# A hybrid encoder block: the memory branch's fourth gate unit moves from the attention phase into the last memory head

## The chip, the cores and the metric

The kernel runs on one core of a Trainium2 chip. The core has five engines with instruction queues of their own: TensorE (PE, matmuls, with its weight loads shown apart as PEld), VectorE (DVE), ScalarE (ACT), GpSimd (POOL) and SyncE (SP, which here only starts transfers). They meet through semaphores. The metric is the device time of one execution in microseconds.

## The reference

The block takes x (1024 tokens, 1024 channels) and a fixed memory of 256 rows. It normalises x and projects it with one wide matrix into everything that follows. Three mixers run side by side, and each is widened with a gate:

```python
h = rms_norm(x, g_pre[layer])
a_qkv, bq, bk, bv, mq, ga, gb, gm, mg = jnp.split(h @ w_in[layer], split_at, axis=-1)
# oa: dilated sliding-window attention, 3 groups x 8 heads of 64
# ob: grouped-query attention, 8 query heads on 2 key heads, softmax over all 1024 keys
sm = jnp.einsum('bshd,bnhd->bhsn', mq.reshape(b, s, M_HEADS, M_HEAD_DIM), km).astype(jnp.float32)
pm = jax.nn.softmax(sm * (M_HEAD_DIM ** -0.5), axis=-1).astype(dt)
om = jnp.einsum('bhsn,bnhd->bshd', pm, vm).reshape(b, s, M_Q)
ya = (oa * jax.nn.silu(ga)) @ w_br_a[layer]
yb = (ob * jax.nn.silu(gb)) @ w_br_b[layer]
ym = (om * jax.nn.silu(gm)) @ w_br_m[layer]
gates = jax.nn.sigmoid((mg + b_merge[layer]).astype(jnp.float32)).astype(dt).reshape(b, s, N_BRANCHES, d)
merged = gates[:, :, 0] * ya + gates[:, :, 1] * yb + gates[:, :, 2] * ym
x = x + rms_norm(merged @ w_out[layer], g_post[layer])
```

The change concerns silu(gm): 512 gate channels of the memory branch, worked out as four units of 128 channels.

## The kernel before

Every float32 matmul is done in three passes. A number is split into a high part (names ending in h) and the rest (ending in l), and high x high, high x low and low x high are added up in PSUM. ACT makes the high part by a copy and DVE the low part by a subtraction (the helper `split`, L105 and L106).

A dense unit projects all 1024 tokens to 128 output channels. It is two halves of 512 tokens, and each half is 24 matmuls of 128x512 (L143, L145, L147), so a unit has 48. Its weights are one transfer of 512 KB (L114), split by ACT (wh) and DVE (wl). A half goes to one of two PSUM tiles named d, and an evacuation empties it. The evacuation of a gate unit (`add_gate`) is a multiplication on DVE (L220), a tanh on ACT (L221), a multiplication on DVE (L222) and a transfer of 256 KB to memory (L223). A filler unit (`add_filler`) has one DVE multiplication (L212), one tanh and one transfer.

The dense units stand in one queue. `weave` takes the next so many units and runs them between the steps of an attention generator. It compares the shares of dense work and attention work that are done, by costs written into the code, and yields to the one that is behind (with a factor called lead). This fixes the order of PE's instructions when the program is built. The other engines' orders come from a scheduler with priorities, and are fixed then too. Each engine works through its own list in order.

The phases, in time: the start with the key and value projections, up to 60 us; the memory phase (M) up to about 225 us; phase B, the grouped-query attention, up to 572 us; phase A, the dilated attention, up to 1150 us; then the merge and the output projection.

In the memory phase `m_att(h)` handles head h of four. Its tokens come in four steps n of 256. A step n has, on PE, the scores (6 matmuls of 128x256 into s), on DVE a minimum (L581) and a small multiplication (L582), on ACT two exponentials (L584), on DVE a reciprocal (L587) and two scalings of pm (L589), then on PE four transposes of pm (L597), a split of the result into mph (ACT) and mpl (DVE), and last 6 matmuls into ov, which ACT copies to om (L611) and SP stores to od. The transposes follow the scores by two steps, the ov matmuls by three. The queries of a head are the tiles mqh and mql, one buffer each.

Phase B opens with `b_const`, on POOL: it writes KB (128 partitions x 2048), from ones (L672, 4 partitions) and from KS (L673, 64 partitions), and a small tile `one` (L674). KB belongs to a pool that lies where the memory phase's pool was, so its first write waits until the tiles there have been read for the last time. `b_att` then runs 16 blocks of 8 steps. A step has on PE one matmul for a row maximum (L688, to tr), two for scores (L706, L707) and two for the product with the values (L727, L728). DVE reduces tr to bn (L689) and makes bpl (L106), ACT makes the exponentials bp (L709) and bph, and POOL sums bp into bl (L716, L718). Once a block DVE makes bnm (L691), PE transposes it (L696), and DVE writes a part of QL from it (L697). With all that go 16 dense units before the change: nine gate units and seven fillers.

Of the kernel before, what the change touches and what calls it, by code (L numbers as in the profile page):

```python
# [50 lines left out]
def block(ctx: ExitStack, tc: tile.TileContext, x, xT, memT, cst, msk, bcst, tabA, gpost,  # L51
# [27 lines left out]
    def pss1():  # L79
        return bank["p"].tile([P, 512], F32, name="s1", tag="s1", bufs=bank["n"][1])  # L80

    def pst():
        return bank["p"].tile([P, 4, 128], F32, name="tr", tag="t", bufs=bank["n"][2])

    def pso():
        return bank["p"].tile([P, 512], F32, name="ov", tag="o", bufs=bank["n"][3])
# [17 lines left out]
    def split(dst_h, dst_l, src):  # L104
        A.activation(dst_h, src, AF.Copy)  # L105
        V.tensor_tensor(dst_l, src, dst_h.bitcast(F32), op=OP.subtract)  # L106
# [3 lines left out]
    def load_w(src, n=1024):  # L110
        if extra:
            extra.append(extra.pop(0))
        raw = (extra[0] if extra else wp).tile([P, 1024], F32, name="wr", bufs=WR)
        nc.sync.dma_start(raw[:, :n], src)  # L114
        wh = wp.tile([P, 1024], R, name="wh")
        wl = wp.tile([P, 1024], R, name="wl")
        split(wh[:, :n], wl[:, :n], raw[:, :n])
        k = n // 128
        return (wh[:, :n].rearrange("p (k f) -> p k f", k=k),
                wl[:, :n].rearrange("p (k f) -> p k f", k=k))  # L120

    def passes(out_ps, terms):
        n = len(terms)
        for i, (a, b) in enumerate(terms):
            PE.matmul(out_ps, a, b, start=i == 0, stop=i == n - 1)  # L125
# [24 lines left out]
    queue = []  # L150
    ready = {}

    early = {}
# [9 lines left out]
    def run_items(count):  # L163
        for _ in range(count):
            n = done[0]
            prepare(n)
            prepare(n + 1)
            yield from queue[n][1](ready.pop(n))
            done[0] += 1

    def cost_items(count):
        return sum(q[2] for q in queue[done[0]:done[0] + count])

    def weave(count, att=None, att_cost=0.0, lead=1.0, prio=ATT_PRIO):
        dg = run_items(count)
        dc = cost_items(count)
        d = a = 0.0
        live_d, live_a = True, att is not None
        while live_d or live_a:
            if live_d and (not live_a or a / att_cost >= min(1.0, d / dc * lead)):  # L180
                try:
                    d += next(dg)
                except StopIteration:
                    live_d = False
                    d = 1e18
            else:
                try:
                    with tc.high_priority(offset=prio):
                        a += next(att)
                except StopIteration:  # L190
                    live_a = False
# [3 lines left out]
    def add_unit(src, evac):  # L195
        def gen(w):
            for half in range(2):
                p = psd()
                yield from dense(w, half, p)
                evac(half, p)  # L200
        queue.append((lambda: load_w(src), gen, UNIT))
# [15 lines left out]
    def add_gate(i, p_):  # L217
        def evac(half, p):
            th = fp["p"].tile([P, 512], F32, name="fth", bufs=2)
            V.tensor_tensor(th, p, rb[:, half * 512:half * 512 + 512], op=OP.mult)  # L220
            A.activation(p, th, AF.Tanh, scale=0.5)  # L221
            V.scalar_tensor_tensor(th, p, 1.0, th, op0=OP.add, op1=OP.mult)  # L222
            nc.sync.dma_start(g2d[i, p_, :, half * 512:half * 512 + 512], th)  # L223
        add_unit(wu[U_G + 4 * i + p_], evac)
# [13 lines left out]
    def close(p):  # L238
        p.__exit__(None, None, None)
# [327 lines left out]
    def m_att(h):  # L567
        qh, ql = MQ[h]
        for _ in range(4):
            yield 250  # L570
        st = {}

        def scores(n):
            sv = pss1().rearrange("p (t k) -> p t k", t=2)
            nm = mt_.tile([P, 2], F32, name="mnm", bufs=3)
            l = mt_.tile([P, 2], F32, name="mls", bufs=3)
            pm = mt_.tile([P, 2, 256], F32, name="pm", bufs=2)
            for j in range(2):
                t = slice((2 * n + j) * 128, (2 * n + j) * 128 + 128)
                passes(sv[:, j], [(qh[:, t], kmh[:, h]), (qh[:, t], kml[:, h]), (ql[:, t], kmh[:, h])])  # L580
            V.tensor_reduce(nm, sv, axis=AX.X, op=OP.min)  # L581
            V.tensor_tensor(nm, nm, rcol[:, 2 * n:2 * n + 2], op=OP.mult)  # L582
            for j in range(2):
                A.activation(pm[:, j], sv[:, j], AF.Exp, scale=nrcol[:, 2 * n + j:2 * n + j + 1], bias=nm[:, j:j + 1],  # L584
                             accum_out=l[:, j:j + 1])
            rl = mt_.tile([P, 2], F32, name="mrl", bufs=4)
            V.reciprocal(rl, l)  # L587
            for j in range(2):
                V.tensor_scalar(pm[:, j], pm[:, j], rl[:, j:j + 1], None, op0=OP.mult)  # L589
            st[n] = pm  # L590

        def trans(n):
            pm = st[n]
            tp = pst().rearrange("p (k t) q -> p k t q", k=2)
            for kt in range(2):
                for j in range(2):
                    PE.transpose(tp[:, kt, j, :], pm[:, j, kt * 128:kt * 128 + 128], ident)  # L597
            ph = mt_.tile([P, 2, 256], R, name="mph", bufs=2)
            pl = mt_.tile([P, 2, 256], R, name="mpl", bufs=2)
            split(ph, pl, tp.rearrange("p k t q -> p k (t q)"))  # L600
            st[n] = (ph, pl)

        def pv(n):
            ph, pl = st.pop(n)
            o = pso()
            terms = []
            for kt in range(2):
                terms += [(vmh[:, kt, h], ph[:, kt]), (vmh[:, kt, h], pl[:, kt]), (vml[:, kt, h], ph[:, kt])]
            passes(o[:, 0:256], terms)
            om = mt_.tile([P, 256], F32, name="om", bufs=2)  # L610
            A.activation(om, o[:, 0:256], AF.Copy)  # L611
            nc.sync.dma_start(od[2, h, :, n * 256:n * 256 + 256], om)

        for n in range(7):
            if n < 4:
                scores(n)
            yield 654
            if 0 <= n - 2 < 4:
                trans(n - 2)
            yield 436  # L620
            if 0 <= n - 3 < 4:
                pv(n - 3)
            yield 654

    M_COST = 1000.0 + 7 * (654 * 2 + 436.0)
# [3 lines left out]
    mq_unit(2)  # L629
    mq_unit(3)  # L630
    add_gate(2, 2)
    early[len(queue)] = lambda: load_w(wu[U_G + 11])
    weave(1)
    weave(2, m_att(0), M_COST, 1.2)
    weave(2, m_att(1), M_COST, 1.2)
    weave(1, m_att(2), M_COST, 1.0)
    weave(1, m_att(3), M_COST, 1.0)
    close(mtp)
    close(mbp)
    close(mlp)  # L640
# [4 lines left out]
    with tc.tile_pool(name="ba", bufs=1, reuse_waits="tile") as ba:  # L645
# [137 lines left out]
        ng = 0  # L783
        for i in (2, 1, 0):
            for p_ in range(4):
                if (i, p_) not in ((2, 0), (2, 1), (2, 2)):
                    add_gate(i, p_)
                    ng += 1
        for j in FILL_B:
# [324 lines left out]
    with tc.tile_pool(name="mg", bufs=1, reuse_waits="tile") as mg:  # L1114
# [78 lines left out]
        for m in range(len(steps) + 2):  # L1193
            if m < len(steps):
                n, i, f = steps[m]
                ths[m] = mg_unit(i, f)
            if m >= 2:
                n, i, f = steps[m - 2]
# [87 lines left out]
U_G = 36  # L1286
# [112 lines left out]
```

## Time and profile before

| what | us |
|---|---|
| median of 3 runs | 1531.39 (1531.35 to 1532.13) |
| the profiled execution | 1529.17 |
| its span, first to last instruction | 1527.2 |
| PE busy in the span | 1493.5 (98%) |
| DVE busy | 966.0 (63%) |
| ACT busy | 713.5 (47%) |
| POOL busy | 429.8 (28%) |

The granted clock of TensorE was 0.997 of its full speed in the mean of the profiled execution. A matmul of 128x512 has a duration of 0.40 us in the records but starts 0.23 us after the one before, since matmuls are pipelined; where work is counted here, the distance of the starts is used. In the lists of the profile a line gives the engine, the line of the kernel, the operation, the output and inputs by name, and their sizes. A bracket or an arrow names what an idle engine waited for. An engine's durations include the time in which a started instruction is held up.

### The profile page before, as it was taken

Reading aid. Unit: us, or ns where it says so; the run is one execution under the profiler, and the core shown is the slowest. Engines: PE = TensorE matmul, PEld = TensorE weight load, DVE = VectorE, ACT = ScalarE, POOL = GpSimd, SP = SyncE. Lnnn points to the kernel's source line nnn. Section 1 sums busy time; section 2 is a strip of 40 time slices with the busy share of each in tenths; the row PEclk is TensorE's granted clock in tenths of the full one; section 3 lists DMA queues with packets and bytes.
Section 4 is the critical chain, followed back from the end, with each engine's and each line's share of the span. In section 5 each row is a group of like instructions: output and inputs, shape, how many; then the busy total and the mean of one; then the engine's idle time right before and its main releaser. Section 6 shows DMA issues by size and latency. Waiting matters only on the chain.

```text
span 1527.2 us, 20804 instructions
## 1 busy us (share of the span) xinstructions
PE 1493.5 (98%) x7748; PEld 1233.9 (81%) x7748; DVE 966.0 (63%) x1602; ACT 713.5 (47%) x1459; POOL 429.8 (28%) x357
## 2 busy tenths in 40 slices
PE   7899989999999999999999999999999999999998
PEld 7799977777777778888878888887888788888787
DVE  7665569999988975555566566556635442524843
ACT  6544345666677661554445445444642111212321
POOL 1425413444444552211221222122200100223422
PEclk9999999999999999999999999999999999999999
DMA  6232011111111112101121121112126541623432
GB/s 233 90 111 70 29 51 57 53 56 49 63 34 60 63 63 87 42 29 43 54 61 43 42 83 45 42 31 83 42 77 195 172 126 35 206 70 117 124 111 97
DMA packets 55044, 119.79 MB, mean 78 GB/s; under 512 B 13792, under 2 KB 23712, under 8 KB 54816
## 3 DMA queue, kind: packets, MB, share of 16 engines
q1 hardware_dynamic: 54800, 118.34, 24.4%
q8 instruction: 61, 1.00, 0.3%
q14 instruction: 39, 0.32, 0.1%
q10 hardware_dynamic: 144, 0.13, 0.0%
HBM read 96.06 MB, written 22.38 MB: 78 GB/s over the span
## 4 chain that ended last, share of the span: by engine, by line
PE 77%; DVE 10%; issue 4%; ACT 4%; POOL 3%; DMA 3%; SPq 0%; DVEq 0%; POOLq 0%; ACTq 0%
PE d L147 12%; PE d L143 12%; PE d L145 12%; PE sc L125 7%; PE sc L1246 4%; PE s L125 3%; PE sc L147 3%; PE sc L143 3%; PE sc L145 3%; PE ov L987 2%; DVE bpl L106 2%; PE ov L728 2%; PE s L707 1%; PE s L706 1%; PE ov L727 1%
## 5 line engine op out<-in xcount | busy, mean ns | idle before, releaser
L143 PE MATMUL d<-hh,wh 128*128 128x512 f32 x992 | 396.4, 400 | 5.2 <-DVE fth L222 5.2
L147 PE MATMUL d<-hh,wl 128*128 128x512 f32 x992 | 397.3, 400 | 0.0
L145 PE MATMUL d<-hl,wh 128*128 128x512 f32 x992 | 393.8, 397 | 0.0
L143 PEld LDWEIGHTS d<-hh,wh 128*128 128x128 f32 x992 | 187.3, 189 | 42.5 <-DVE fth L222 6.5
L147 PEld LDWEIGHTS d<-hh,wl 128*128 128x128 f32 x992 | 187.3, 189 | 39.0 <-issue 4.0
L145 PEld LDWEIGHTS d<-hl,wh 128*128 128x128 f32 x992 | 187.4, 189 | 36.2 <-issue 1.0
L105 ACT ACTIVATE wh<-wr 128x1024 fp32r<-128x1024 f32 (+1 forms) x100 | 95.3, 954 | 245.4 <-PE sc L145 106.0
L718 POOL TENSOR_TENSOR bl<-bl,bp 128x512 f32<-128x512 f32 x96 | 135.8, 1414 | 121.3 <-ACT bp L709 111.2
L836 POOL TENSOR_TENSOR rot<-rot,t2a 128x512 f32<-128x512 f32 x48 | 82.5, 1720 | 297.6 <-DVE t2a L835 297.6
L106 DVE TENSOR_TENSOR bpl<-bp,bph 128x512 fp32r<-128x512 f32 x128 | 131.9, 1031 | 23.6 <-ACT bph L105 23.1
L106 DVE TENSOR_TENSOR wl<-wr,wh 128x1024 fp32r<-128x1024 f32 (+1 forms) x100 | 119.0, 1190 | 21.5 <-ACT wh L105 20.8
L709 ACT ACTIVATE bp<-s 128x512 f32<-128x512 f32 x128 | 76.2, 595 | 59.9 <-PE s L707 57.8
L1147 POOL TENSOR_TENSOR acc<-acc,th 128x1024 f32<-128x1024 f32 x16 | 45.4, 2837 | 201.5 <-DVE th L1146 201.5
L945 ACT ACTIVATE pra<-pra,sts 128x128 f32<-128x128 f32 (+2 forms) x152 | 67.1, 442 | 62.3 <-DVE sts L937 61.6
L689 DVE TENSOR_REDUCE bn<-tr 128x1 f32<-128x512 f32 x128 | 86.5, 680 | 3.8 <-PE tr L688 3.3
L147 PE MATMUL sc<-hh,wl 128*128 128x512 f32 x224 | 87.3, 390 | 1.2 <-DVE wl L106 1.2
L937 DVE CUSTOM_DVE_ANT_0 pra<-s,mask 128x128 f32<-128x128 f32 (+2 forms) x152 | 48.4, 348 | 62.2 <-PE s L125 49.2
L143 PE MATMUL sc<-hh,wh 128*128 128x512 f32 x224 | 87.3, 390 | 0.0
L145 PE MATMUL sc<-hl,wh 128*128 128x512 f32 x224 | 87.1, 389 | 0.0
L105 ACT ACTIVATE bph<-bp 128x512 fp32r<-128x512 f32 x128 | 80.8, 631 | 3.5
L833 DVE TENSOR_TENSOR rot<-d,tab 128x512 f32<-128x512 f32 x48 | 33.1, 689 | 67.4 <-PE d L147 67.1
L125 PE MATMUL sc<-gh,wh 128*128 128x512 f32 x192 | 74.7, 389 | 0.0
(276 smaller groups left out, 3066.0 us busy)
## 6 DMA issues: line engine op xcount, KB each, us to landing
wr<-in_wu SPq DMA_DIRECT2D x76, 512.0 KB
g2d<-fth SPq DMA_DIRECT2D x24, 256.0 KB
wgt<-wgd SPq DMA_DIRECT2D x24, 256.0 KB
ot<-od SPq DMA_DIRECT2D x12, 512.0 KB
gt<-g2d SPq DMA_DIRECT2D x12, 512.0 KB
wr<-in_wbr SPq DMA_DIRECT2D x24, 256.0 KB
thd<-fth SPq DMA_DIRECT2D x20, 256.0 KB
th<-thd SPq DMA_DIRECT2D x10, 512.0 KB
```

The lines of the kernel that those rows point to most:

```text
L105: A.activation(dst_h, src, AF.Copy)
L106: V.tensor_tensor(dst_l, src, dst_h.bitcast(F32), op=OP.subtract)
L125: PE.matmul(out_ps, a, b, start=i == 0, stop=i == n - 1)
L143: PE.matmul(dst, wh[:, k, :], hh[k][:, t], start=k == 0, stop=False)
L145: PE.matmul(dst, wh[:, k, :], hl[k][:, t], start=False, stop=False)
L147: PE.matmul(dst, wl[:, k, :], hh[k][:, t], start=False, stop=k == 7)
L689: V.tensor_reduce(st[i]["n"][:, j, c:c + 1], s, axis=AX.X, op=OP.min)
L709: A.activation(pp, s, AF.Exp, scale=-1.0)
L718: G.tensor_tensor(lsum[i % 2], lsum[i % 2], pp, op=OP.add)
L836: G.tensor_tensor(o[:, t], o[:, t], t2, op=OP.add)
L945: A.activation(src, raw, AF.Exp, scale=-1.0, bias=bias, accum_out=sts[:, h, 1, T:T + 1])
L1246: PE.matmul(parts[h], *terms[h][j], start=j == 0, stop=j == 23)
```

## The change

The fourth gate unit of the memory branch, (2, 3), is put into the queue behind (2, 2). The last head's `weave` takes two units instead of one, so (2, 3) is now done between the steps of `m_att(3)`. Phase B's list leaves out all of branch 2, and has 15 dense units instead of 16. The weights that are loaded ahead of phase B are now those of gate unit (1, 0), its new first unit.

```diff
     mq_unit(2)
     mq_unit(3)
     add_gate(2, 2)
-    early[len(queue)] = lambda: load_w(wu[U_G + 11])
+    add_gate(2, 3)
+    early[len(queue)] = lambda: load_w(wu[U_G + 4])
     weave(1)
     weave(2, m_att(0), M_COST, 1.2)
     weave(2, m_att(1), M_COST, 1.2)
     weave(1, m_att(2), M_COST, 1.0)
-    weave(1, m_att(3), M_COST, 1.0)
+    weave(2, m_att(3), M_COST, 1.0)
     close(mtp)
...
         for i in (2, 1, 0):
             for p_ in range(4):
-                if (i, p_) not in ((2, 0), (2, 1), (2, 2)):
+                if i < 2:
                     add_gate(i, p_)
                     ng += 1
```

## The prediction

> **What bounds the kernel now.** I read the busy shares first, then PE's waits, then the stretch where the longest of them falls, and last the two stretches of the phase that gives the unit up.
>
> ```profile
> PE 1493.5 (98%) x7748; PEld 1233.9 (81%) x7748; DVE 966.0 (63%) x1602; ACT 713.5 (47%) x1459; POOL 429.8 (28%) x357
> ```
>
> TensorE (PE) is busy for 98% of the span, so 33.7 of 1527.2 us are idle, and a change of order that leaves the matmuls as they are can only move idle time and the clock. The table of who PE waited for (total, times, longest) says where the idle time is:
>
> ```profile
> PE tr L597 <- DVE pm L589: 4.2, 2, 2.6
> PE s L707 <- DVE QL L697: 2.0, 4, 0.8
> ...
> PE ov L728 <- DVE bpl L106: 1.5, 3, 0.7
> ...
> PE tr L696 <- DVE bn L689: 1.2, 2, 0.7
> ```
>
> Line 1 is in the last memory head; the others, with 1.3 us for fth at 415 us, are phase B. The head's stretch in order of time (start, duration, engine, line):
>
> ```profile
> 208.64 0.28 PE L125 MATMUL s<-kmh,mql 128*128 128x256 f32 x1
> 209.08 5.39 POOL L672 TENSOR_SCALAR KB<-ones 4x2048 fp32r<-4x2048 f32 x1 [35.00 <-PE s L125]
> 210.23 6.34 DVE L589 TENSOR_SCALAR pm<-pm,mrl 128x256 f32<-128x256 f32 x2
> 214.54 1.88 POOL L673 CAST KB<-KS 64x2048 fp32r<-64x2048 f32 x1
> 214.77 0.30 PE L597 MATMUL tr<-cs,pm 128*128 128x128 f32 x1 [2.60 <-DVE pm L589]
> 216.50 0.15 DVE L582 TENSOR_TENSOR mnm<-mnm,rcol 128x2 f32<-128x2 f32 x1
> 216.63 0.90 PE L597 MATMUL tr<-cs,pm 128*128 128x128 f32 x3 [1.55 <-DVE pm L589]
> ```
>
> The stall isn't for lack of dense work. When the head's last score matmul has read the queries (208.9), POOL is free to write phase B's KB into their place. While POOL's two copies run (209.08 to 216.42), two VectorE (DVE) scalings that elsewhere take 0.62 us together take 6.34: the first ends with the first copy, the second with the second. PE idles 2.60 + 1.55 + 0.31 = 4.46 us for them. Then its clock is low (0.80 granted in the mean of 212.0 to 220.4, below): until 219.7 the 128x256 matmuls start 0.21 us apart, before the stall 0.12. From 212.01 to 220.35 PE does 4 transposes (0.36 us), 6 ov (0.71) and 3 dense matmuls (3 x 0.232): 1.77 us of work in 8.34. The stall's whole price is 6.57 us, 4.46 idle and 2.11 slow.
>
> The last view is of stretches (PE, PEld, DVE, ACT, POOL busy): the stall, phase B up to its last gate unit, phase B with its fillers.
>
> ```profile
> 212.00:220.40 8.40, 3.93 (x15) 2.98 (x15) 7.26 (x9) 2.35 (x7) 4.55 (x3) 0.80 0.14 49
> 225.00:433.00 208.00, 203.11 (x880) 158.33 (x879) 194.35 (x257) 138.90 (x230) 89.96 (x65) 1.00 0.17 54
> 433.00:572.00 139.00, 137.76 (x598) 108.37 (x597) 121.16 (x149) 95.28 (x155) 69.65 (x49) 1.00 0.17 56
> ```
>
> In phase B DVE is nearly as full as PE: 93.4% with 2.35% of PE idle in the first part, 87.2% with 0.9% in the second.
>
> **The change, part by part.** Lines are those of before; in after the numbers are one higher from L633 on.
>
> *The moved unit.* 48 dense matmuls of 0.232 us = 11.1 us, one 512 KB weight load, its split on ACT and DVE, two evacuations (L220, L221, L222) and two 256 KB stores. All of it is still done once: the head's stretch grows by 11.1 us of PE, phase B shrinks by 11.1, sum 0.
>
> *The stall in the last head.* Nothing in the edit touches KB's place or POOL's order, so POOL starts 0.3 us after the last scores as before and is busy for 7.3 us. What changes is what DVE has in front of it then. I walk it from T = 0, the end of the last scores (n=3), in the order of each engine's instructions in the changed kernel, with before's durations.
> - PE: 5 dense, transposes of n=1, 3 dense, ov of n=0, 9 dense, transposes of n=2, 3 dense = 20 x 0.232 + 2 x 0.36 + 0.71: it reaches ov of n=1 at T = 6.1.
> - DVE has done pm of n=2 by T = -0.4, since twice as much dense work stands between the scores. So the wait of line 1 of PE's table goes. Next on DVE: the minimum of n=3 (0.68), L220 (0.67), L582 (two inputs, 128x2, at T = 1.4), the weight split wl (1.22), L222, the reciprocal, pm of n=3, and only then mpl of n=1 (0.69), for which ov of n=1 waits.
> - If L582 is held until the first copy ends (T = 5.7), ACT's two exponentials of n=3 behind it run from 5.9 to 7.2, and mph of n=1, behind them on ACT, is there at 7.9. On DVE wl and POOL's second copy go one behind the other. With the copy first, wl ends at 8.8, L222 at 9.4, pm at 10.2 and mpl at 10.8; with wl first, pm waits for the copy until 8.7 and mpl ends at 10.0.
> - PE then stands at ov of n=1 from 6.1 to 10.0 or 10.8, but for one matmul at 7.9: 3.9 to 4.7 us, mean 4.3. The slow clock follows a stall of this size again; 2.0 us by the 2.11 of before. Price 6.3 for 6.57: **-0.3 us**. What is late next: the transposes of n=3 come 3 us after ov of n=1, when pm is done.
>
> Is L582 held? Rows speak on both sides (the first gives minimum, median and maximum in ns):
>
> ```profile
> L691 DVE TENSOR_TENSOR bnm<-bn x16: 151/932/1242, 236.2 to 545.2; 128x4 f32<-128x4 f32 x16
> 273.26 0.97 DVE L691 TENSOR_TENSOR bnm<-bn 128x4 f32<-128x4 f32 x1
> 272.91 1.30 POOL L718 TENSOR_TENSOR bl<-bl,bp 128x512 f32<-128x512 f32 x1 [1.32 <-ACT bp L709]
> 118.20 0.15 DVE L582 TENSOR_TENSOR mnm<-mnm,rcol 128x2 f32<-128x2 f32 x1
> 117.61 1.02 POOL L315 TENSOR_TENSOR ssb<-ssb,mhalf 128x4 f32<-128x4 f32 x1
> ```
>
> L691, as small and with two inputs too, takes 151 ns alone and 0.97 under POOL's 128x512 add, ending with it. Under POOL's power of 128x4 L582 isn't held; but that reads four elements a row, and KB's copy reads 2048. I take L691's case. wl, of the same kind, is held in phase B (1.47 us in the mean, 1.22 elsewhere). If neither were held and pm alone were, pm would end at 7.8, mpl at 8.5: a stall of 2.4 us with a slow clock of 0 to 2.0, or **-4.2 to -2.2**. At the other end, both pieces long and the clock low for as long again: 4.7 + 2.5 = 7.2, **+0.6**.
>
> The Trainium skill ("SBUF — State Buffer", section "Who interferes with whom") says that a VectorE instruction with two SBUF inputs contends with a GpSimd instruction that reads SBUF, and that the second one to issue blocks until the first has finished. By it L582 and wl are held, as taken above; L691 agrees with it, and L582 at 118.2 us doesn't, so no run here settles it for KB's copy. By the page the sum would stay at -0.3; by the row at 118.2 us it would be -2.2 or less.
>
> *Phase B with one dense unit less under the same attention.* Its 347 us become 335.9. DVE loses 4 evacuation steps (0.6 us each back to back) and one wl (1.4): 315.5 - 3.8 = 311.7 busy, so its share goes from 90.9 to 92.8%. The two parts of phase B give the price of a share: 6.2 points of DVE more went with 1.45 points of PE idle, 0.234 per point. 1.9 points x 0.234 = 0.45% of 336 us = **+1.5 us**. A second reading agrees: a step of the attention gets 3.3% shorter (2.53 to 2.45 us), so the results that were late, two or three steps after their inputs, are late by 0.16 to 0.24 us more, 10 times: +1.6 to 2.4. Ends: from 345 to 405 us PE has no idle time at DVE shares of 90 to 95%, so by chance of alignment the 6.1 us of before could shrink (-2); the worst 20 us (285 to 305) have 1.1 us idle, and if 8 gate units (185 us) ran so and the fillers at 2.35%, idle were 10.2 + 3.5 = 13.7, +7.6. I take 1.5, the mean of the two parts.
>
> *Queues.* The unit's two stores stand on SP between the head's four od stores, and one weight load ahead of them waits for wl (T = 8.8). The output tile that needs the first od store back is written at T = 15, some 6 us later: nothing, unless wl is later still. POOL's order doesn't change. The load of the next unit goes early in both kernels: nothing.
>
> **Sum.** -0.3 + 1.5 = +1.2 us. The profiled execution took 1529.17 us (span 1527.2), 2.2 below the median of 1531.39: 1530.4 on its scale, 1532.6 on that of the runs.
>
> **Rivals.**
> - *Phase B is bound by DVE.* For: in the gate part its share would go from 93.4 to some 95%, and the highest 20 us reach 97%. Against it: a late DVE finds POOL done, and bpl then takes 0.68 us, not 1.22, so backlogs drain. It decides once idle in phase B grows by over 3.4 us; at +6 with -0.3: 1537.1, slower.
> - *The stall goes.* More dense work per score was to give DVE time, and for pm of n=2 it does. For: POOL could start later, or mpl run ahead of pm. Against: the order on DVE puts mpl behind it. -6.6 + 1.5: 1526.3, faster.
> - *Only pm is held.* -3.2 + 1.5: 1529.7, no change.
>
> **How the numbers follow.** 0.2% (3.06 us) is about what a measurement of this kernel can tell from no change. Forecast 0.52, only pm held 0.11, stall gone 0.11, phase B bound by DVE 0.26. Faster 0.12 (the third, and a hundredth of the second's tail), slower 0.30 (the last and 0.04 of the forecast's tail), same 0.58. The range leaves out the stall gone and tails: 1529.0 (only pm held, less 0.7) to 1537.1.
>
> **What would show it.** In the profile after: PE's wait for pm at L597 small or gone, and a wait of ov at L125 for mpl or mph of 3 to 5 us in its place; L582 or wl with a duration of over 4 us under KB's copy; the granted clock low behind it; the waits of phase B at 7 to 8 us, on the same lines as before; DVE at 92 to 93% there. I am wrong if L582 takes 0.15 us under the copy, or if phase B's waits come to 10 us or below 5.

## The result, and the profile after

Two sets of runs compare the kernels. In the first, after takes 1528.15 us (median of 7, 1525.65 to 1528.54) and before 1531.40 (median of 7): a ratio of 0.9969, 95% interval 0.9958 to 0.9981. In a second set, the first experiment below, the ratio is 0.9982, interval 0.9973 to 0.9990. The change makes the kernel faster by 0.2 to 0.3%, some 3 us. The forecast was 1532.6, no change to be measured, with a range from 1529.0: wrong in its sign, and the median is 0.85 us below the range.

The first profiled execution of after, the fastest of its seven, takes 1525.65 us with a span of 1523.8, 3.5 us less than the one of before. Its table of PE's waits (total, times, longest; lines are one higher from L633 on):

```profile
PE s L370 <- ACT hh L271: 6.4, 1, 6.4
PE d L143 <- DVE fth L222: 3.9, 2, 3.2
PE ov L729 <- DVE bpl L106: 2.7, 2, 1.9
PE ov L125 <- DVE mpl L106: 2.2, 1, 2.2
PE s L707 <- ACT bp L710: 1.9, 3, 1.4
...
PE s L708 <- DVE QL L698: 1.3, 2, 0.7
```

The transposes' wait for pm (4.2 us in before) is gone. One wait of 2.2 us has come in its place, at the ov matmuls of n=1. The same stretch in order of time:

```profile
210.99 0.62 DVE L589 TENSOR_SCALAR pm<-pm,mrl 128x256 f32<-128x256 f32 x2
211.69 5.39 POOL L673 TENSOR_SCALAR KB<-ones 4x2048 fp32r<-4x2048 f32 x1 [40.27 <-DVE pm L589]
212.77 2.58 DVE L582 TENSOR_TENSOR mnm<-mnm,rcol 128x2 f32<-128x2 f32 x1
215.28 1.21 DVE L106 TENSOR_TENSOR wl<-wr,wh 128x1024 fp32r<-128x1024 f32 x1
217.15 1.89 POOL L674 CAST KB<-KS 64x2048 fp32r<-64x2048 f32 x1
217.27 2.18 DVE L589 TENSOR_SCALAR pm<-pm,mrl 128x256 f32<-128x256 f32 x2
219.37 0.68 DVE L106 TENSOR_TENSOR mpl<-tr,mph 128x512 fp32r<-128x512 f32 x1
220.10 0.38 PE L125 MATMUL ov<-mpl,vmh 128*128 128x256 f32 x1 [2.23 <-DVE mpl L106]
```

The first pm (n=2) is done before POOL starts. L582 takes 2.58 us and not 0.15, so POOL's copy does hold it, but it comes free at 215.35, 3.66 us after the copy's start, and the copy goes on to 217.08. The weight split wl then runs its ordinary 1.21 us wholly under the copy. The second pm is held by the second copy (2.18 us for 0.62).

**Where the 3.5 us of this pair lie.** I cut the span at three of PE's starts, and put the 11.12 us of the moved unit where before has them.

| profile | start to the fourth query unit | from there to phase B's first transposes, less moved units | phase B to the 25th dense unit, plus moved units | rest of the span | stretches of half clock before the end, at us |
|---|---|---|---|---|---|
| before | 181.61 | 43.84 | 360.64 | 941.2 | 56, 217 |
| before, again | 178.96 | 45.60 | 360.68 | 941.2 | 214 (twice as long) |
| after | 178.96 | 41.24 | 361.47 | 942.2 | 221 |
| after, again | 182.87 | 39.68 | 363.12 | 942.5 | 55 (twice as long), 383 |

In the first pair 2.65 us of the difference come before anything that the change touches, 2.60 in the memory heads, and phase B gives 0.8 back. The second pair has it the other way round in the first column. So the first column is chance, and the second one and the third are the change. The rest of the span is 1.0 to 1.3 us longer in after, where PE, DVE, ACT and POOL have the same instructions in the same order. PE's waits there make 0.8 of it (4.3 and 4.5 us in before, 5.1 and 5.3 in after). The three profiles of held kernels below that have no slow stretch there take 941.2 to 943.1 us for these same instructions, so I can't count it to the change; what makes it stays open.

### The profile page after: what moved, and what is told of

It reads as the page before. It is cut to its first block, busy times and chain, and to the rows that moved or that the text cites. A ratio compares the mean times of both kernels' runs of the same rounds, so it can differ in the third digit from the quotient of the medians.

```text
span 1523.8 us, 20817 instructions
## 1 busy us (share of the span) xinstructions
PE 1491.9 (98%) x7748; PEld 1233.6 (81%) x7748; DVE 961.3 (63%) x1602; ACT 713.0 (47%) x1459; POOL 425.2 (28%) x357
## 4 chain that ended last, share of the span: by engine, by line
PE 77%; DVE 8%; ACT 4%; issue 4%; DMA 3%; POOL 3%; SPq 0%; DVEq 0%; POOLq 0%; ACTq 0%
PE d L147 12%; PE d L145 12%; PE d L143 12%; PE sc L125 7%; PE sc L1247 4%; PE s L125 3%; PE sc L147 3%; PE sc L143 3%; PE sc L145 3%; PE ov L988 2%; PE ov L729 2%; PE s L708 2%; PE s L707 2%; PE ov L728 1%; PE tr L689 1%
## 5 line engine op out<-in xcount | busy, mean ns | idle before, releaser
L719 POOL TENSOR_TENSOR bl<-bl,bp 128x512 f32<-128x512 f32 x96 | 130.5, 1360 | 114.3 <-ACT bp L710 110.5
```

Source lines behind the costliest of these rows:

```text
L719: G.tensor_tensor(lsum[i % 2], lsum[i % 2], pp, op=OP.add)
```

## The experiments

They ran in three sets, each beside the kernel before. Its median was 1530.40 in the first two sets and 1529.63 in the last, which has the fill in before and the second pair of held kernels.

**Both kernels again.** No edit.

> The kernel before, once more, for a second profile. In the first profiles after was 3.5 us shorter, but 2.65 us of that came before 200 us, where the two kernels have the same instructions: before had a stretch of half clock at 56 us and after had none. Theory 'the start is chance': the transposes of macc fall anywhere from 61.0 to 63.4 us here too, with no tie to the kernel, and the time is 1529 to 1534.5. Theory 'the start belongs to the kernel': they fall at 63.3 again, with half clock at 56 us.

> The kernel after, once more. The head's stretch should repeat: one wait of 2.2 us at ov of n=1, L582 held 2.6 us and not to the end of the first copy, half clock for 3.4 us behind it, 2.6 us less lost than in before. By 'the start is chance' the median difference to before is the head's -2.6 and phase B's +0.8, so about -2 with a start that varies on both sides; by 'the start belongs to the kernel' macc falls at 61.0 again and the difference is -3.3 or more.

Measured: before 1529.97 (11 runs, 1526.60 to 1532.14), ratio 0.9996 (0.9988 to 1.0005) to itself; after 1527.02 (11 runs, 1525.68 to 1529.97), ratio 0.9982 (0.9973 to 0.9990). PE's transposes of the tile macc (L258), at the end of the start, stand at 63.3 and 61.0 us in the two profiles of before, at 61.0 and 64.1 in those of after: the start is chance. What makes the chance is the clock. The windows from 50 to 62 us of before, before again, after and after again (columns as in the prediction's last view; the third figure from the right is the granted clock):

```profile
50.00:62.00 12.00, 8.79 (x32) 6.76 (x32) 9.47 (x20) 6.29 (x12) 7.08 (x8) 0.86 0.30 88
50.00:62.00 12.00, 8.80 (x42) 6.84 (x41) 9.54 (x19) 6.59 (x13) 6.37 (x7) 1.00 0.30 88
50.00:62.00 12.00, 8.80 (x43) 6.86 (x42) 9.52 (x19) 6.56 (x13) 6.34 (x7) 1.00 0.28 88
50.00:62.00 12.00, 8.80 (x26) 6.67 (x25) 8.95 (x18) 5.77 (x11) 6.63 (x7) 0.72 0.29 88
```

PE is busy for 8.8 us in each, and does 32, 42, 43 and 26 matmuls in them: the same program gets none, one or two stretches of half clock of 3.4 us there. Over all thirteen profiles of this document the fourth query unit starts at 178.96 us with none of them, at 180.5 to 181.6 with one and at 182.2 to 182.9 with two. The head repeats in its waits to 0.1 us (L582 held 2.58 us, the wait 2.23), but not in its clock: after again has no slow stretch behind the wait, and before again has two behind its own. A stretch costs half its length: 45.60 - 43.84 = 1.76 us for one more, 41.24 - 39.68 = 1.56 for one less.

What decides is where a wait falls. In each profile the slow stretches before the end begin and end on a grid of 3.41 us, which lies elsewhere in every execution. From 12 us on, in all thirteen profiles, each step of the grid in which PE is idle for 1.9 us or more is followed by half clock, and none with 1.8 or less is; of three between them (1.81, 1.85, 1.88) the first is. Once slow, the clock stays so for another step if 0.66 us or more of the step is idle, and recovers at 0.43 or less. In after the step from 217.6 us holds the whole wait of 2.23; in after again an edge at 222.2 cuts the same wait into 0.4 and 1.8, and no slow stretch follows. The wait of 1.95 us for bpl is cut in after and lies whole in one step in after again, where half clock follows. The four steps, two of after and two of after again (PE's busy time stands behind the length):

```profile
217.65:221.06 3.41, 1.18 (x9) 0.94 (x9) 3.00 (x4) 0.36 (x2) 1.58 (x2) 1.00 0.69 254
378.07:381.49 3.41, 2.12 (x9) 1.76 (x10) 3.38 (x6) 0.12 (x1) 0.69 (x1) 1.00 0.49 154
222.21:225.62 3.41, 1.61 (x10) 1.44 (x11) 2.34 (x4) 0.38 (x1) 0.92 (x2) 1.00 0.59 209
379.22:382.63 3.41, 1.47 (x7) 0.91 (x6) 3.41 (x4) 1.17 (x2) 1.27 (x1) 1.00 0.54 191
```

**POOL's copies held back in before.** POOL's first copy takes its factor of -1 from a small tile, neg1 (neg in the profile), which DVE writes behind the last head's last scaling.

```diff
+            if h == 3 and n == 3:
+                V.tensor_scalar(neg1, pm[:, 1, 0:1], 0.0, -1.0, op0=OP.mult, op1=OP.add)
...
-            G.tensor_scalar(KB[64:68], ones[64:68, :, None].to_broadcast([4, 2, S]), -1.0, None, op0=OP.mult)
+            G.tensor_scalar(KB[64:68], ones[64:68, :, None].to_broadcast([4, 2, S]), neg1[64:68], None, op0=OP.mult)
```

> Before, with POOL's copies to KB made to wait for the last pm of the last head (a number that they multiply by is made from that pm by one more DVE instruction; no other instruction is moved). Theory 'the port': the stall at L597 is made by the copies alone, pm takes 0.62 us for two, the waits there and the half clock go, 6.6 us less than before: about 1524.8. Rival 'too little dense work': with one unit in the head the chain from scores to transposes is too long by itself, PE still waits 2 us or more at L597: 1528 to 1531. Rival 'moved cover': the copies run later and hold phase B's first DVE work, waits at L688 or L707 of 2 to 4 us come in their place: 1527 to 1529.

Measured: 1523.72 (5 runs), ratio 0.9953 (0.9939 to 0.9966). PE has no wait in the head, and no other instruction was moved on any engine. The scalings of n=2 and n=3 and the copy in this kernel:

```profile
210.11 0.61 DVE L590 TENSOR_SCALAR pm<-pm,mrl 128x256 f32<-128x256 f32 x2
212.48 0.62 DVE L590 TENSOR_SCALAR pm<-pm,mrl 128x256 f32<-128x256 f32 x2
213.48 5.47 POOL L675 TENSOR_SCALAR KB<-ones,neg 4x2048 fp32r<-4x2048 f32 x1 [39.77 <-DVE neg L592]
```

From 204 to 216 us PE is busy all the time (behind the window stand its length and PE's busy time):

```profile
204.00:216.00 12.00, 12.00 (x75) 10.43 (x74) 8.70 (x25) 8.02 (x23) 2.52 (x1) 1.00 0.21 76
```

The stretch of the heads takes 37.51 us, 6.3 less than in before's first profile and 8.1 less than in its second. So with one dense unit in the last head, as in before, PE is busy without a pause: the stall was the copies alone, and the rival 'too little dense work' falls. So does 'moved cover': phase B up to the 25th dense unit takes 359.8 us here, 0.9 less than in before, so the copies cost PE nothing that shows where they now run.

**The same in after.** The edit is the same, in after.

> After, with the same hold of POOL's copies. Theory 'the port': after's wait of 2.2 us at ov of n=1 and the 1.7 us of half clock go, 3.9 us less than after: 1524 to 1525, and no better than b_hold, since phase B's 0.8 us stay: b_hold is the faster by 0 to 2 us. Rival 'the change is worth something by itself' (the extra dense work in the head is needed): a_hold is faster than b_hold by 2 us or more.

Measured: 1522.38 (5 runs), ratio 0.9947 (0.9935 to 0.9960), below the 1524 to 1525 expected; the heads 37.20 us, no wait in them. The two held kernels are 1.3 us apart the other way than 'the port' had it, within both intervals, so both were run again, side by side.

> Before with POOL's copies held, again, on one chip with the next. With the stall gone in both, what is left of the change is phase B's price: theory 'only the stall made the gain' has this one level with a_hold2 or the faster by up to 1 us (1523 to 1524).

> After with POOL's copies held, again. By 'only the stall made the gain' it is level with b_hold2 or slower by up to 1 us; by 'the moved unit is worth something of its own' it is faster by 1 us or more, as the medians of the first pair (1522.4 and 1523.7) would have it.

Measured: 1523.72 (0.9943 to 0.9970) and 1523.61 (0.9947 to 0.9972), 5 runs each. They are level. Once the copies no longer meet the scalings, the moved unit makes no difference that these runs can tell. What the change gained, it gained on that stall. Level totals are not level stretches, though: the heads take 37.5 us in the held before and 37.2 in the held after, both times, while phase B takes 359.8 and 359.6 against 361.2 twice. So a moved unit costs phase B 1.4 to 1.6 us there, and the rest of the span, with the same instructions in both, gives it back in these profiles (943.1 and, with a slow stretch at 1437 us, 944.0 against 941.4 and 941.2); why stays open.

**The unit in the third head.** After's queue, with the second unit one head earlier.

```diff
-    weave(1, m_att(2), M_COST, 1.0)
-    weave(2, m_att(3), M_COST, 1.0)
+    weave(2, m_att(2), M_COST, 1.0)
+    weave(1, m_att(3), M_COST, 1.0)
```

> After's queue (phase B with 15 units), but the second unit is woven with the third memory head and the last head has one unit, as in before. Theory 'the port': POOL's copies meet the scalings of the last head as in before, PE waits 4.2 us at L597 with a slow clock behind it; phase B costs its 0.8 to 2.4 us more: 1531 to 1533, 0.5 to 2.5 above before. Rival 'dense work per head': one more unit anywhere in the memory phase gives its waits cover, so this is as fast as after, 1527.

Measured: 1533.65 (11 runs), ratio 1.0019 (1.0010 to 1.0027): slower than before, by 3.25 us in the medians, above the 0.5 to 2.5 expected. PE's waits in this kernel have before's line again:

```profile
PE tr L597 <- DVE pm L589: 4.2, 2, 2.6
PE d L143 <- DVE fth L222: 3.9, 2, 3.2
PE ov L729 <- DVE bpl L106: 2.7, 2, 2.0
...
PE s L707 <- ACT bp L710: 1.9, 3, 1.4
```

One more unit in the memory phase doesn't help by itself. It has to stand in the last head, where it changes what DVE does while POOL copies. Without that the stall stays (the heads take 45.98 us, with two slow stretches, as in before again), and phase B's price is added: 363.07 us, with a slow stretch at 387, as in after again. A further slow stretch, at 1193 us, lengthens this profile.

**The scaling with two tensors as inputs, in before.**

```diff
-                V.tensor_scalar(pm[:, j], pm[:, j], rl[:, j:j + 1], None, op0=OP.mult)
+                V.tensor_tensor(pm[:, j], pm[:, j], rl[:, j:j + 1].to_broadcast([P, 256]), op=OP.mult)
```

> Before, with the scaling of pm as a multiplication of two tensors (the reciprocal broadcast along the row) in place of a tensor by a number for each row. Theory 'read and write halves are held apart': the form with two inputs is held by POOL's reading alone, so the first pm under KB's copy ends 3.7 us after the copy's start in place of 5.4 and the second follows at once; PE's wait at L597 falls from 4.2 to 1 to 1.8 us: 1526 to 1528.5. Rival 'held for the whole instruction': both end as in before, 1530.

Measured: 1525.82 (9 runs), ratio 0.9973 (0.9962 to 0.9983). It is a little below the 1526 to 1528.5 expected. A copy to om on ACT, and its transfer, now stand ahead of the last head's last two exponentials, so before's wait of 0.31 us for om is gone as well; on DVE a minimum and its multiplication moved up in two places, at 117 and 158 us, outside the last head.

```profile
208.21 5.40 POOL L672 TENSOR_SCALAR KB<-ones 4x2048 fp32r<-4x2048 f32 x1 [34.67 <-PE s L125]
209.36 3.12 DVE L589 TENSOR_TENSOR pm<-pm,mrl 128x256 f32<-128x256 f32 x2
212.29 0.79 PE L597 MATMUL tr<-cs,pm 128*128 128x128 f32 x4 [0.99 <-DVE pm L589]
213.67 1.89 POOL L673 CAST KB<-KS 64x2048 fp32r<-64x2048 f32 x1
214.09 2.09 DVE L589 TENSOR_TENSOR pm<-pm,mrl 128x256 f32<-128x256 f32 x2
215.99 0.79 PE L597 MATMUL tr<-cs,pm 128*128 128x128 f32 x4 [0.76 <-DVE pm L589]
```

Both scalings of n=2 are done at 212.48, 1.1 us before the copy from ones ends (213.61); in before the first of them ended with that copy and the second with the next. PE's wait at L597 falls from 4.2 to 1.8 us. Under the copy of KS the same form is held until that copy ends (215.56): this copy holds it to the end.

**KB's first part filled instead of multiplied, in after and in before.**

```diff
-            G.tensor_scalar(KB[64:68], ones[64:68, :, None].to_broadcast([4, 2, S]), -1.0, None, op0=OP.mult)
+            G.memset(KB[64:68].bitcast(F32), -1.0)
```

> After, with KB's first part written by a fill with the constant -1 in place of a multiplication of ones, so that POOL reads nothing for it. Theory 'read and write halves of the port are held apart': L582 and wl, which have two inputs and write through the ordinary port, take 0.15 and 1.2 us under the fill; pm is held only if the fill or the second copy is still running when its turn comes. With a fill of 5 us POOL is free at 7.3 us after the last scores as before and the wait at ov of n=1 stays at 1 to 2.2 us: 1525.5 to 1527. With a fill of 1 to 2 us both writes are over before pm of n=3: no wait, 1522 to 1524. Rival 'one lock for all': L582 ends with the fill, and the wait at ov changes only as the fill is shorter.

> Before, with KB's first part written by the fill that reads nothing (1.81 us where the multiplication took 5.39). Theory 'two halves': the scaling pm, which also uses the port that POOL writes through, is held by the fill to 2.1 us after the last scores though the fill reads nothing, and its second instruction by the copy of KS to 4.0 us; PE's wait at L597 falls from 4.2 to 0.5 to 1.5 us, about 1524.5. Rival 'only reads hold': pm of n=2 is done before the copy of KS begins and PE doesn't wait at L597 at all, 1523.

Measured in after: 1523.76 (6 runs), ratio 0.9956 (0.9944 to 0.9969), no wait in the head.

```profile
213.81 1.81 POOL L673 MEMSET KB<- 4x2048 f32 x1 [40.20 <-DVE pm L589]
214.94 0.15 DVE L582 TENSOR_TENSOR mnm<-mnm,rcol 128x2 f32<-128x2 f32 x1
215.06 1.23 DVE L106 TENSOR_TENSOR wl<-wr,wh 128x1024 fp32r<-128x1024 f32 x1
215.68 2.35 POOL L674 CAST KB<-KS 64x2048 fp32r<-64x2048 f32 x1
217.09 1.36 DVE L589 TENSOR_SCALAR pm<-pm,mrl 128x256 f32<-128x256 f32 x2
```

L582 takes 0.15 us under the fill, and wl starts under it without waiting. It is now the copy of KS that is held, by wl: 2.35 us for 1.89. Measured in before: 1523.97 (5 runs), ratio 0.9965 (0.9952 to 0.9977), a wait of 0.7 us at L597 and one of 0.9 for om:

```profile
207.94 1.80 POOL L672 MEMSET KB<- 4x2048 f32 x1 [34.95 <-PE s L125]
209.13 2.71 DVE L589 TENSOR_SCALAR pm<-pm,mrl 128x256 f32<-128x256 f32 x2
209.80 1.89 POOL L673 CAST KB<-KS 64x2048 fp32r<-64x2048 f32 x1
211.89 0.55 PE L597 MATMUL tr<-cs,pm 128*128 128x128 f32 x3 [0.70 <-DVE pm L589]
```

Two scalings that nothing holds take 0.61 us and would have been over at 209.74, before the copy of KS began. They end at 211.84, 0.15 us after that copy. The first alone ends at 209.89, 0.15 us after the fill. So the first was held by the fill, which reads nothing, to 209.74, and the second by the copy: 'two halves' is borne out, 'only reads hold' falls. The form with two inputs is held by POOL's reading, the scaling also by its writing.

**A second unit out of phase B.** After, with gate unit (1, 0) in the last head as well and (2, 2) in the third; phase B has 14 units.

```diff
     add_gate(2, 3)
-    early[len(queue)] = lambda: load_w(wu[U_G + 4])
+    add_gate(1, 0)
+    early[len(queue)] = lambda: load_w(wu[U_G + 5])
...
-    weave(1, m_att(2), M_COST, 1.0)
+    weave(2, m_att(2), M_COST, 1.0)
...
-                if i < 2:
+                if i < 2 and (i, p_) != (1, 0):
```

> After, with one more unit out of phase B: gate unit (1, 0) goes to the last head too, (2, 2) to the third, so phase B has 14 units. Theory 'DVE's share in phase B has a price': each unit taken out costs phase B 0.8 to 2.4 us, the head stays as in after: 1528 to 1529.5. Rival 'phase B has slack, its price in after was chance': 1526.5 to 1527.5. Rival 'DVE bound': the second unit costs much more than the first, 1531 or more.

Measured: 1537.23 (7 runs, 1533.19 to 1541.08), ratio 1.0043 (1.0027 to 1.0059), 10 us above after. The heads take 40.72 us, as in after. Phase B, with the two units put back, takes 370.08: 8.6 more than after's 361.47, which was 0.8 more than before's. That is the outcome that the rival 'DVE bound' named. PE's waits in phase B of this kernel:

```profile
PE s L708 <- ACT bp L711: 4.9, 7, 1.6
PE s L709 <- DVE QL L699: 3.3, 5, 1.0
PE tr L125 <- DVE bll L106: 1.2, 1, 1.2
PE d L143 <- DVE fth L222: 1.1, 1, 1.1
```

The price of a unit isn't a slope: the first costs 0.8 us (1.4 to 1.6 between the held kernels), the second 8.6. In after a wait of PE for ACT's exponentials (1.9 us) had come up that before doesn't have; with 14 units it is the longest. But DVE's share of phase B is 91.0% here and 90.8% in after, so the rival has the price and not the reason; what makes these results late wasn't tried.

## Why the prediction was wrong

**What bounds the kernel: right.** The stall at L597 was made by POOL's copies and by nothing else; holding them back removes it with every other order kept (1523.72 for 1530.40).

**The moved unit, the queues: right.** PE has 2976 dense matmuls in both kernels, and no wait of the stores or loads came up.

**The stall in the last head: the place right, the size wrong.** The wait at L597 went, one at ov of n=1 came, L582 was held, pm was held by the second copy, the clock was low behind it. The step that failed is "If L582 is held until the first copy ends (T = 5.7)" and with it "On DVE wl and POOL's second copy go one behind the other". On its time scale (T = 0 at 211.37) L582 was free at 4.0, and wl was done at 5.1, under the copy and ahead of the second one. So mpl came at 8.7 and not at 10.0 to 10.8, and PE waited 2.2 us and not 3.9 to 4.7. The Trainium skill ("SBUF — State Buffer", section "Who interferes with whom") has the one that comes first hold the shared ports for its whole instruction. That is what I priced. For the scaling pm it holds (in before to the end of the copy's 5.39 us); for the form with two inputs the trace differs: 3.66 us of the copy's 5.39. My reason for the hold was that KB's copy reads 2048 elements a row; it reads one element of ones a row, 2048 times over. Whether that is why it lets go early wasn't tried. The measurement decides, and the same section's other rule, that this form meets only POOL's reads, is what the fill shows (0.15 us).

**The slow clock: a number that should have been a spread.** I set 2.0 us for both kernels. Before lost one or two stretches in its two profiles, after one or none, at 1.6 to 1.8 us each. Against the 37.2 us of the held kernel the heads lose 6.6 and 8.4 us in before, 4.0 and 2.5 in after. The term "-0.3" is -2.6 in the first pair and -4.3 in the mean of both. The end of its range, -4.2, was the case that I gave 0.11, "only pm is held": the wait of 2.4 us that goes with it is the one that came, by another way.

**Phase B: right in sign and near in size, by luck.** +1.5 was forecast; +0.8 was measured without a slow stretch, 2.4 with one at 383 us, and 1.4 to 1.6 between the held kernels. But the step behind it, that DVE's share goes up by 1.9 points and that each point has a price, failed. The windows from phase B's first transposes to the next phase's first dense unit, before and after (PE, PEld, DVE, ACT, POOL busy):

```profile
225.45:575.21 349.76, 343.63 (x1488) 269.01 (x1487) 315.86 (x405) 234.35 (x385) 159.60 (x113) 1.00 0.17 55
231.32:570.79 339.47, 332.62 (x1440) 260.46 (x1439) 308.14 (x400) 231.91 (x382) 155.22 (x113) 1.00 0.16 54
```

DVE's share goes from 90.3 to 90.8%, since DVE does 7.7 us less and not 3.8: the 16 small bnm instructions, held by POOL, took 13.6 us and now take 9.8. At my price 0.5 points are 0.4 us. The next unit out of phase B, in the kernel with 14, adds 0.3 points and 8.6 us. "On the same lines as before" was wrong, too: waits for DVE at QL and bnm became shorter (3.2 us to 1.9), the one for fth (1.3) went, those for bpl became longer (1.5 to 2.7), and ACT's exponentials came in (1.9). In all PE waits 6.8 us there, for 6.0 in before.

**The sum.** -0.3 + 1.5 gave no change. With the measured terms, -4.3 in the heads and +0.8 to +2.4 in phase B, it is -3.5 to -1.9; the rest of the span takes back 1.0 to 1.3. The runs show -3.25 by the medians of the first set and -2.8 by the ratio of the second. Four profiles close this sum to 1 or 2 us, no better: the second one of after was the slowest of its 11 runs. I gave faster 0.12 because the only way to it that I priced was the stall going altogether. A shorter stall was priced as no change, though at -1.7 it needed 1.4 us more to count.

**The version that beats both.** Holding the copies back (1523.7 in before, 1522.4 and 1523.6 in after) or filling KB (1523.8 and 1524.0) gains about twice what the change does; with either the unit can stay where it was.

## What to carry to other kernels

Before more work is put beside a stall, look at which instruction ran ten times its usual time (6.34 us for 0.62) and what ran on the engine beside it: here two copies of POOL on another phase's behalf, set free by a buffer, were the whole of it. One false dependence removed it, and a fill most of it. When an instruction is held by another engine's, price the hold from both ends, the other's first release and its last, and let both ends carry a chance. A slope taken between two parts of a phase is a guess until a run shows that its variable moves: here the share moved by a quarter of what was forecast, and the price of the next step was 8.6 us.

## What the runs showed of the hardware

- A VectorE instruction with two inputs in SBUF was held by a GpSimd multiplication of a broadcast column for 3.66 us after its start, a scaling by a number per row for all of its 5.39 us. Under a copy that reads 2048 different elements a row (1.89 us), the first form was held to the end as well. Whether it is the broadcast that lets it go earlier wasn't tried.
- The same 4x2048 write takes GpSimd 5.39 us as a multiplication and 1.81 us as a fill.
- The clock falls to half for stretches of 3.4 us, or two of them, and the same program has them in one execution and not in the next: none, one or two at 55 us, behind the head's stall, at 383 us behind a wait of 1.95 for bpl. Each costs 1.6 to 1.8 us in the heads. By an estimate they make most of the 5.5 us by which runs of one kernel differ: 1526.60 ran at a mean clock of 0.998 and 1532.14 at 0.995, and 0.003 of 1527 us is 4.6. The Trainium skill ("TensorE: Matmul & The Clock Gate", section "Part 1: The HAM clock gate") gives a free-running window of 3413 ns and a clock of one half behind an idle one; the length and the level agree. An idle window it need not be: some 1.9 of 3.41 us were enough here (1.90, 1.95 and 2.23 us were followed by half clock, 1.80 was not).
